# Layer 0's attention scores in the "b" banks, and a shorter given time after the delta rule's first two steps

## The chip, the cores and the metric

The kernel runs on one core of a Trainium2 chip. The metric is device time in microseconds for one execution of the whole program. The engines are TensorE (PE in the profile), VectorE (DVE), ScalarE (ACT), GpSimd (POOL) and SyncE (SP, which issues the DMAs). TensorE runs at one of two clock levels, 2.4 or 1.2 GHz; the profile gives the granted level as a share of full speed.

## What is computed

A trunk of two layers works on 256 tokens of width 2048. Each layer normalises its input, shifts and scales it by a vector computed from a condition (the "ada" product), projects it once into the inputs of three groups of heads, runs the groups, and maps their gated outputs back by one output projection.

```python
for l in range(DEPTH):
    shift, scale, gate = jnp.split(c_act @ w_ada[l] + b_ada[l], 3, axis=-1)
    h = rms_norm(x, norm_w[l]) * (1.0 + scale[:, None, :]) + shift[:, None, :]
    (gq, gk, gv, glr, gz, dq, dk, dv, da, db, dz, aq, ak, av, az) = jnp.split(h @ w_in[l], bounds, axis=-1)
    ...
    o_gla = gla_chunked(...)                  # gated linear attention, 4 heads
    ...
    o_gdn = gated_delta_chunked(...)          # gated delta rule, 4 heads, chunks of 64 tokens
    ...
    q_d = apply_rope(q_d, cos_b, sin_b)
    k_d = apply_rope(k_d, cos_b, sin_b)
    o_diff = diff_attention(q_d, k_d, v_d, lam)   # softmax(q1 k1) - lam * softmax(q2 k2), causal, 4 heads
    ...
    y = jnp.concatenate([o_gla, o_gdn, o_diff], axis=-1) @ w_out[l]
    x = x + gate[:, None, :] * y
```

Each group's output is normalised per head and multiplied by a silu gate (`z` in the kernel) ahead of the concatenation.

## The kernel before

**The main work.** Weights come from HBM in pieces of 128 x 1024 floats. ACT casts each piece to a rounded form `wh` (line 309), DVE takes the difference `wl` (line 311), and TensorE multiplies with both, three matmuls for a product: these are the matmuls into `pt`, `pf` (the input projection, `project`) and `py` (the output projection, `out_project`). DVE also makes the ada products of layer 1 during layer 0 (line 327, on pieces that a DMA brings). The output projection has three parts: the first takes the linear attention's gated output (192 matmuls), the second the delta rule's (192), the third the differential attention's (384). A part can't start until its group's gate is done (`run_until`). I call the place between two parts a barrier. Matmuls into `pt`, `pf` and `py` together are "the projection's matmuls" in what follows.

**The side work.** The three groups of heads are written as generators: `gla`, `gdn` (the delta rule), `diff_qk` (rotary step of queries and keys), `diff_attend` (scores, softmax, products), and `gate_out` (gate, transposes, split). `poll` calls them between the projection's matmuls. A generator yields either a condition or a given time `YW[i]`, in microseconds of a model clock that counts TensorE's work as it is written; it goes on when the clock is that much later. A scheduler then places each engine's instructions by a simulated timeline, with the generators' instructions at a high priority; so a given time changes the order on every engine, of instructions that lie far behind it too.

`gdn`: first, for each of the two token tiles, transposes and normalises the keys, and yields `YW[8]` behind each (line 748). Then come decays, the inverse of a triangular matrix in five levels (`Y_ps`, `Z_ps` on TensorE; DVE's lines 809 and 812; POOL's line 799), the products of queries and keys (`QK_ps`, line 795), then u and w, and the recurrence over four chunks: `wS_ps`, line 876 (`vn`), `S_ps`, line 888 (`S_gdn`). The outputs `o_gdn` of a token tile are copied by ACT (line 903), squared (line 563), and then seven POOL instructions follow one another: lines 907, 908, 909, 376 (a power), 911, 912, and 1036 of `gate_out`.

`diff_qk`: the rotary step multiplies by tables (lines 939 and 941, into the scratch `scr`), adds (line 943), and TensorE transposes the result into `ropeT_ps`. The scratch is shared with the linear attention, whose norm reads it in line 660 on POOL (after lines 657 and 376), once per token tile.

`diff_attend`: for each head and token tile a tile of scores `s_ps`, which leaves PSUM by lines 967 (DVE) and 969 (ACT), the softmax (lines 971 to 983), transposes `aT_ps` (line 989), products `o_diff`, and five small POOL instructions on `r_o` (lines 999 to 1003). Up to two tiles run at a time.

`gate_out`: line 1036 multiplies by the gate, TensorE transposes into `oT_ps`, ACT (line 1046) and DVE (line 1047) split the result for `py`.

**PSUM.** Eight banks have three tags: four of tag "p" for the projections, two of tag "a" and two of tag "b". The delta rule takes "a". The linear attention, the rotary transposes, `aT_ps` and `o_diff` take "b". `s_ps` and `oT_ps` take "a" when `free_a()` says that all of the delta rule has been written, and "b" otherwise; `free_a` speaks of what has been written, not of what has run.

Of the kernel before, what the change touches and what calls it, by code (L numbers as in the profile page):

```python
# [28 lines left out]
RAW = 1024  # L29
RAWS = 6  # L30

YW = {0: 7.0, 1: 8.0, 2: 25.0, 3: 1.25, 4: 2.0, 5: 2.0, 6: 15.0, 7: 2.5, 8: 11.25, 9: 3.25, 10: 6.0, 11: 4.0, 12: 2.94, 13: 0.75, 14: 1.5, 15: 3.0, 16: 3.0, 17: 3.5, 18: 2.0, 19: 3.75, 20: 6.25, 21: 7.5, 22: 3.75, 23: 10.0, 24: 14.0, 25: 0.75, 26: 3.75, 27: 7.0, 28: 2.25, 29: 12.0, 30: 4.2}


_SPLITS = (("gq", 256), ("gk", 256), ("gv", 512), ("glr", 16), ("gz", 512), ("dq", 512), ("dk", 512), ("dv", 512),
# [109 lines left out]
def hybrid_trunk(ctx: ExitStack, tc: tile.TileContext, x, cvec, pos, par, w_ada, w_in, w_out, w_lr, qkn, adt, cst, out):  # L145
# [23 lines left out]
    def bank(name, tag):  # L169


        return psum.tile([P, 512], F32, name=name, tag=tag, bufs=BANKS[tag])

    def tiny(name, n, bufs=2):
        return small.tile([P, n], F32, name=name, tag=name, bufs=bufs)
# [6 lines left out]
    def mm(o, lhsT, rhs, start=True, stop=True, fast=False, **kw):  # L182
        clock[0] += rhs.shape[-1] * (0.00042 if fast else 0.0017)
        return PE.matmul(o, lhsT=lhsT, rhs=rhs, start=start, stop=stop, **kw)  # L184

    def transpose(o, i):
        clock[0] += 0.11
        PE.transpose(out=o, in_=i, identity=ident)
# [82 lines left out]
    def cc(name, n=128, off=0):  # L271
        return ct[:, CST[name] + off:CST[name] + off + n]
# [102 lines left out]
    def row_power(o, v, n):  # L375
        POOL.tensor_tensor(o, v, mhalf[:, 0:n], ALU.pow)
# [170 lines left out]
    def heads(ap, n=4):  # L547
        return ap.rearrange("p (h d) -> p h d", h=n)

    def over_heads(ap, n=4, d=128):  # L550
        return ap.rearrange("p (o d) -> p o d", o=1).broadcast_to([P, n, d])
# [6 lines left out]
    def head_norm(src, n, width, r):  # L558

        for h in range(n):  # L560
            a = junk_n[0] % (256 // width) * width
            junk_n[0] += 1
            ACT.activation(junk[:, a:a + width], src[:, width * h:width * h + width], AF.Square, accum_out=r[:, h:h + 1])


    def gla(l, o, on, scr):
# [4 lines left out]
        SP.dma_start(wlr, w_lr[l])  # L571
        yield YW[0]
        pb = bank("lrT", "b")
# [3 lines left out]
        ACT.copy(lrT, pb[0:16, 0:T])  # L577
        yield YW[1]
        pz = bank("la_ps", "b")
# [21 lines left out]
        DVE.tensor_tensor(ke, gk, enb, ALU.mult)  # L601
        yield YW[2]
        pk = bank("ktT_ps", "b")
# [6 lines left out]
        for t in range(2):  # L610
            attT.append(scr[:, 4 + t])
            POOL.memset(attT[t], 0.0)
            for u in range(2):
                yield YW[3]
                pa = bank("att_ps", "b")
# [6 lines left out]
        for n in range(3):  # L622
            t, f = n // 2, 64 * (n % 2)
            yield YW[4]
            pd = bank("dS_ps", "b")
# [11 lines left out]
        for t in range(2):  # L637
            raw = scr[:, 2 * t]
            for u in range(2):
                yield YW[5]  # L640
                po = Bank(bank("o_gla", "b"))
# [311 lines left out]
    def diff_attend(l, o, g, on, scr, free_a):  # L953
        causal = cc("causal")
        qT = lambda t, i: o.aqk[:, t, 0, 128 * i:128 * i + 128]
        kT = lambda t, i: o.aqk[:, t, 1, 128 * i:128 * i + 128]
        yield YW[22]

        def one_tile(h, t, turn):
            W = 128 * (t + 1)  # L960
            pb = bank("s_ps", "a" if free_a() else "b")
            for m in range(2):
                for k in range(t + 1):
                    mm(pb[:, W * m + 128 * k:W * m + 128 * k + 128], qT(t, 2 * h + m), kT(k, 2 * h + m))
            s = scr[:, (1 + turn) % 7]
            sv, pv = heads(s[:, 0:2 * W], 2), heads(pb[:, 0:2 * W], 2)
            DVE.tensor_tensor(sv[:, :, W - 128:W], pv[:, :, W - 128:W], over_heads(causal, 2), ALU.add)
            if t == 1:
                ACT.copy(sv[:, :, 0:128], pv[:, :, 0:128])
            mxs = tiny("mx_s", 2)  # L970
            DVE.tensor_reduce(mxs, sv, AX.X, ALU.max)
            sc = g.sq[t][:, 2 * h:2 * h + 2]
            nb = tiny("nb", 2)
            DVE.scalar_tensor_tensor(nb, mxs, -1.0, sc, ALU.mult, ALU.mult)
            sm = tiny("sm", 2)
            for m in range(2):
                ACT.activation(sv[:, m, :], sv[:, m, :], AF.Exp, bias=nb[:, m:m + 1], scale=sc[:, m:m + 1],
                               accum_out=sm[:, m:m + 1])
            rsm = tiny("rsm", 2, 4)
            DVE.reciprocal(rsm, sm)  # L980
            cf = tiny("cf", 1)
            DVE.scalar_tensor_tensor(cf, sm[:, 0:1], nlam[:, l:l + 1], rsm[:, 1:2], ALU.mult, ALU.mult)
            DVE.scalar_tensor_tensor(sv[:, 0, :], sv[:, 1, :], cf, sv[:, 0, :], ALU.mult, ALU.add)
            yield YW[23]
            pa = bank("aT_ps", "b")
            for k in range(t + 1):
                transpose(pa[:, HS[k]], sv[:, 0, HS[k]])
            aT = scr[:, 7, 256 * (turn % 2):256 * (turn % 2) + 256]
            ACT.copy(aT[:, 0:W], pa[:, 0:W])
            yield YW[24]  # L990
            po = bank("o_diff", "b")[:, 0:256]
            for k in range(t + 1):
                mm(po, aT[:, HS[k]], o.av[:, k, 256 * h:256 * h + 256], k == 0, k == t)
            d = o.aqk[:, t, 0, 256 * h:256 * h + 256]
            ACT.copy(d, po)
            r = tiny("r_o", 1, 4)
            head_norm(d, 1, 256, r)
            rs = rsm[:, 0:1]
            POOL.tensor_tensor(r, r, rs, ALU.mult)
            POOL.tensor_tensor(r, r, rs, ALU.mult)  # L1000
            POOL.tensor_scalar(r, r, 1.0 / 256.0, EPS, ALU.mult, ALU.add)
            row_power(r, r, 1)
            POOL.tensor_tensor(r, r, rs, ALU.mult)
            DVE.tensor_scalar(d, d, r, None, ALU.mult)
            yield YW[25]

        running = []
        todo = [(h, t) for h in range(4) for t in range(2)]
        turn = 0
        while todo or running:  # L1010
            if todo and len(running) < 2:
                h, t = todo.pop(0)
                running.append([clock[0], one_tile(h, t, turn)])
                turn += 1
            item = min(running, key=lambda r: r[0])
            if item[0] > clock[0]:
                yield item[0] - clock[0]
                continue
            w = next(item[1], None)
            if w is None:  # L1020
                running.remove(item)
            else:
                item[0] = clock[0] + w
        for t in range(2):
            on[t] = o.aqk[:, t, 0, :]
# [64 lines left out]
    with tc.issue_after(last_fold.ins), tc.issue_after(squared.ins), tc.issue_after(spread.ins):  # L1090
# [3 lines left out]
        pb = bank("lam_ps", "a")  # L1094
# [11 lines left out]
    for l in range(L):  # L1106
# [78 lines left out]
        def free_a():  # L1185
            return run["gdn"]["done"]
# [184 lines left out]
```

## Time and profile before

| | us |
|---|---|
| three runs | 1104.52, 1107.8, 1108.89 |
| median | 1107.8 |
| the profiled execution's own time | 1106.04 |
| its span in the profile | 1103.9 |
| TensorE busy in the span | 1045.9 (95%) |
| DVE busy | 892.6 (81%) |
| ACT busy | 604.2 (55%) |
| POOL busy | 219.5 (20%) |
| mean granted clock of TensorE | 0.982 |

Times in the rows are counted from the span's start. Layer 0's projection runs up to about 434, its output projection from there to 578, and layer 1 behind it. A row of the timeline gives the start and the length of an instruction or of a run of like ones; in brackets at its end stands how long the engine was idle ahead of it, and which instruction ended that.

### The profile page before, as it was taken

The page shows a single profiled execution, that of the slowest core. Times are in us where ns is not written, and L with a number is a line of the kernel's source. Part 1 is how long each engine was busy: PE and PEld are TensorE (multiplying, and loading weights), DVE is VectorE, ACT ScalarE, POOL GpSimd, SP SyncE. Part 2 cuts the span into 40 slices and gives each one's busy share as a digit, 9 for nine tenths or more (in the row PEclk, how much of TensorE's full clock was granted, in tenths as well). Part 3 has the DMA queues.
Part 4 walks back from the last instruction along what each step waited for, and adds up shares of the span by engine and source line. Part 5 has one row for each costly group of instructions (what it writes and reads, how often), then busy time and mean ns, then how long its engine had stood idle before and what let it go on. Part 6 is the DMA issues. An engine that isn't in the chain of part 4 may idle for free.

```text
span 1103.9 us, 19674 instructions
## 1 busy us (share of the span) xinstructions
PE 1045.9 (95%) x7398; PEld 915.2 (83%) x7398; DVE 892.6 (81%) x1373; ACT 604.2 (55%) x1244; POOL 219.5 (20%) x279
## 2 busy tenths in 40 slices
PE   5989999999899989969898999999999999999998
PEld 5769888888898868959796777899899877889998
DVE  7899999989999878759768687676856878687974
ACT  4845544447655726446545555458554556557642
POOL 0000000040210941133430000014232244202400
PEclk9999999999999989969998999999999999999999
DMA  9989999988977646744578898796544656677462
GB/s 366 348 280 343 340 332 337 317 312 320 317 253 249 192 148 225 269 144 142 165 247 293 319 341 307 262 301 229 180 125 159 212 181 198 223 244 238 134 210 96
DMA packets 76799, 273.24 MB, mean 248 GB/s; under 512 B 8816, under 2 KB 9888, under 8 KB 76576
## 3 DMA queue, kind: packets, MB, share of 16 engines
q1 hardware_dynamic: 76416, 271.80, 71.8%
q8 instruction: 58, 0.95, 0.3%
q14 instruction: 37, 0.30, 0.1%
q10 hardware_dynamic: 288, 0.19, 0.1%
HBM read 267.76 MB, written 4.19 MB: 246 GB/s over the span
## 4 chain that ended last, share of the span: by engine, by line
PE 61%; DVE 16%; DMA 10%; issue 7%; ACT 3%; POOL 2%; DVEq 0%; ACTq 0%; POOLq 0%; SPq 0%
PE pt L184 30%; PE py L184 14%; PE pf L184 8%; DMA rawa<-in_w_ada 7%; DVE wl L311 5%; DVE rawa L327 4%; DMA raw<-in_w_in 2%; ACT wh L309 1%; PE Z_ps L184 1%; PE s_ps L184 1%; PE o_diff L184 1%; PE Y_ps L184 1%; PE o_gla L184 1%; DVE fr L327 1%; DVE on_gdn L673 1%
## 5 line engine op out<-in xcount | busy, mean ns | idle before, releaser
L309 ACT CAST wh<-raw 128x1024 fp32r<-128x1024 f32 (+2 forms) x310 | 318.0, 1028 | 283.4 <-PE pt L184 131.5
L311 DVE TENSOR_TENSOR wl<-raw,wh 128x1024 fp32r<-128x1024 f32 (+2 forms) x310 | 382.1, 1238 | 60.6 <-ACT wh L309 57.6
L184 PE MATMUL pt<-wl,hh 128*128 128x512 f32 (+1 forms) x768 | 293.0, 384 | 4.6 <-DVE wl L311 4.5
L327 DVE SCALAR_TENSOR_TENSOR rawa<-rawa,c_row 128x1024 f32<-128x1024 f32 x184 | 228.3, 1245 | 80.5 <-DMA rawa<-in_w_ada 79.4
L184 PE MATMUL pt<-wh,hl 128*128 128x512 f32 (+1 forms) x768 | 288.8, 380 | 1.2 <-DVE hl L403 1.2
L184 PE MATMUL pt<-wh,hh 128*128 128x512 f32 (+1 forms) x768 | 271.4, 383 | 8.4 <-ACT hh L401 4.3
L184 PEld LDWEIGHTS pt<-wh,hh 128*128 128x128 f32 x768 | 144.5, 190 | 40.8 <-ACT hh L401 5.3
L184 PEld LDWEIGHTS pt<-wl,hh 128*128 128x128 f32 x768 | 145.5, 190 | 39.2 <-DVE wl L311 10.6
L184 PEld LDWEIGHTS pt<-wh,hl 128*128 128x128 f32 x768 | 145.5, 190 | 30.1 <-DVE hl L403 2.0
L184 PE MATMUL pf<-hh,wl 128*128 128x256 f32 x512 | 143.8, 284 | 4.3 <-DVE wl L311 4.3
L184 PE MATMUL pf<-hh,wh 128*128 128x256 f32 x512 | 144.5, 283 | 1.5 <-ACT wh L309 1.5
L184 PE MATMUL pf<-hl,wh 128*128 128x256 f32 x512 | 145.4, 285 | 0.0
L184 PEld LDWEIGHTS pf<-hh,wl 128*128 128x128 f32 x512 | 96.2, 189 | 6.6 <-DVE wl L311 5.3
L184 PE MATMUL py<-ogg,wh 128*128 128x256 f32 x512 | 98.4, 288 | 0.8 <-DVE z L454 0.8
L184 PEld LDWEIGHTS pf<-hh,wh 128*128 128x128 f32 x512 | 97.1, 190 | 2.5 <-ACT wh L309 1.7
L184 PEld LDWEIGHTS pf<-hl,wh 128*128 128x128 f32 x512 | 96.9, 189 | 2.1 <-issue 1.3
L184 PE MATMUL py<-odf,wh 128*128 128x256 f32 x512 | 88.6, 278 | 2.0 <-ACT odf L1046 1.7
L184 PEld LDWEIGHTS py<-ogg,wh 128*128 128x128 f32 x512 | 80.3, 189 | 2.2 <-DVE z L454 1.2
L184 PEld LDWEIGHTS py<-odf,wh 128*128 128x128 f32 x512 | 77.3, 188 | 2.9 <-ACT odf L1046 2.1
L339 ACT ACTIVATE ada_j<-ada_p,pt 128x2 f32<-128x2 f32 x96 | 31.3, 326 | 79.2 <-DVE rawa L327 75.3
L184 PE MATMUL py<-ogg,wl 128*128 128x256 f32 x256 | 72.0, 283 | 0.0
L184 PE MATMUL py<-odf,wl 128*128 128x256 f32 x256 | 70.6, 277 | 0.0
(277 smaller groups left out, 1340.9 us busy)
## 6 DMA issues: line engine op xcount, KB each, us to landing
raw<-in_w_in SPq DMA_DIRECT2D x224, 512.0 KB, 4.9
rawa<-in_w_ada SPq DMA_DIRECT2D x184, 512.0 KB, 4.7
raw<-in_w_out SPq DMA_DIRECT2D x64, 512.0 KB, 4.4
raw<-in_w_in SPq DMA_DIRECT2D x20, 402.0 KB, 4.4
fr<-in_w_ada SPq DMA_DIRECT2D x8, 512.0 KB, 9.2
xt<-in_x SPq DMA_DIRECT2D x4, 512.0 KB, 5.8
xr<-in_x SPq DMA_DIRECT2D x4, 512.0 KB, 7.0
xs<-xr SPq DMA_DIRECT2D x1, 2048.0 KB, 7.2
```

Source lines behind the costliest of these rows:

```text
L184: return PE.matmul(o, lhsT=lhsT, rhs=rhs, start=start, stop=stop, **kw)
L309: ACT.copy(wh, raw)
L311: DVE.tensor_tensor(wl, raw, wh.bitcast(F32), ALU.subtract)
L327: DVE.scalar_tensor_tensor(raw, raw, 1.0, cb, ALU.mult, ALU.mult, accum_out=sums[:, i:i + 1])
L339: ACT.activation(tiny("ada_j", 2), sums[:, 2 * f:2 * f + 2], AF.Identity, bias=bias, scale=scale, accum_out=o)
L673: DVE.scalar_tensor_tensor(yi[:, s:T], src[:, 0:T - s], pcol("conv", w + 3 - s), yi[:, s:T], ALU.mult, ALU.add)
```

## The change

Two edits. The given time `YW[8]` goes from 11.25 to 4.0; it is yielded twice in each layer, at the end of the delta rule's two first steps. And in layer 0 a score tile takes a "b" bank always; in layer 1 it takes what it took before.

```diff
-YW = {0: 7.0, ..., 7: 2.5, 8: 11.25, 9: 3.25, ...}
+YW = {0: 7.0, ..., 7: 2.5, 8: 4.0, 9: 3.25, ...}
...
         def one_tile(h, t, turn):
             W = 128 * (t + 1)
-            pb = bank("s_ps", "a" if free_a() else "b")
+            pb = bank("s_ps", "a" if l > 0 and free_a() else "b")
             for m in range(2):
                 for k in range(t + 1):
                     mm(pb[:, W * m + 128 * k:W * m + 128 * k + 128], qT(t, 2 * h + m), kT(k, 2 * h + m))
```

No instruction is added or taken away; what changes is the order on the engines and the banks. On TensorE the two orders are the same up to the products of queries and keys of layer 0's delta rule, about 377 us in the trace. TensorE there, before (`QK_ps` and `Y_ps` of the delta rule, then the projection's matmuls into `pt`):

```order
L184 MATMUL pt<-wh,hh 128x512
L184 MATMUL pt<-wl,hh 128x512
L184 MATMUL QK_ps<-fm 64x64 x16
L184 MATMUL Y_ps<-Um,C 64x64 x16
L184 MATMUL pt<-wh,hl 128x512
L184 MATMUL pt<-wh,hh 128x512
```

and now:

```order
L184 MATMUL Y_ps<-Um,C 64x64 x12
L184 MATMUL pt<-wh,hl 128x512
L188 MATMUL ropeT_ps<-ct,scr 128x128 x8
L184 MATMUL pt<-wh,hh 128x512
L184 MATMUL pt<-wl,hh 128x512
```

The first rotary transposes stand one projection matmul behind the Y step; before, 43 of these later, between the matmuls of the next Y step. POOL at the same place, before:

```order
L657 TENSOR_SCALAR ss_gla<-ss_gla 128x4
L376 TENSOR_TENSOR ss_gla<-ss_gla,mhalf 128x4
L660 TENSOR_TENSOR mix<-scr,ss_gla 128x512
L924 TENSOR_SCALAR r_d<-r_d 128x8
L376 TENSOR_TENSOR r_d<-r_d,mhalf 128x8
L924 TENSOR_SCALAR r_d<-r_d 128x8
L376 TENSOR_TENSOR r_d<-r_d,mhalf 128x8
L831 TENSOR_TENSOR fm<-fm,ecb 128x4x128
L657 TENSOR_SCALAR ss_gla<-ss_gla 128x4
L797 MEMSET fm 128x1024
L831 TENSOR_TENSOR fm<-fm,ecb 128x4x128
L376 TENSOR_TENSOR ss_gla<-ss_gla,mhalf 128x4
```

(line 799 and the second line 660 follow) and now:

```order
L657 TENSOR_SCALAR ss_gla<-ss_gla 128x4
L376 TENSOR_TENSOR ss_gla<-ss_gla,mhalf 128x4
L657 TENSOR_SCALAR ss_gla<-ss_gla 128x4
L660 TENSOR_TENSOR mix<-scr,ss_gla 128x512
L376 TENSOR_TENSOR ss_gla<-ss_gla,mhalf 128x4
L924 TENSOR_SCALAR r_d<-r_d 128x8
L660 TENSOR_TENSOR mix<-scr,ss_gla 128x512
L376 TENSOR_TENSOR r_d<-r_d,mhalf 128x8
```

The second line 660 comes third behind the first and no longer eleventh. TensorE at the barrier between the first and the second part of layer 0's output projection, before (`S_ps`, `wS_ps`, `o_gdn` of the delta rule's last steps; `s_ps`, `aT_ps`, `o_diff` of the attention; `oT_ps` of the delta rule's gate):

```order
L184 MATMUL S_ps<-vn,kn 128x128 x4
L184 MATMUL wS_ps<-S_gdn,wT 64x128 x4
L184 MATMUL o_gdn<-vn,E 64x128 x8
L184 MATMUL o_gdn<-S_gdn,fm 64x128 x8
L184 MATMUL s_ps<-aqk 128x128 x6
L188 MATMUL oT_ps<-ct,z 128x128 x2
L188 MATMUL aT_ps<-ct,scr 128x128
L188 MATMUL oT_ps<-ct,z 128x128 x6
L188 MATMUL aT_ps<-ct,scr 128x128 x2
L184 MATMUL o_diff<-av,scr 128x256
L184 MATMUL py<-ogg,wh 128x256 x4
```

and now, from the middle of it:

```order
L184 MATMUL s_ps<-aqk 128x128 x6
L184 MATMUL o_gdn<-vn,E 64x128 x7
L184 MATMUL o_gdn<-S_gdn,fm 64x128 x8
L188 MATMUL oT_ps<-ct,z 128x128 x2
L188 MATMUL aT_ps<-ct,scr 128x128 x2
L184 MATMUL o_diff<-av,scr 128x256
L188 MATMUL aT_ps<-ct,scr 128x128
L184 MATMUL s_ps<-aqk 128x128 x2
L184 MATMUL o_diff<-av,scr 128x256 x2
L184 MATMUL s_ps<-aqk 128x128 x4
L188 MATMUL oT_ps<-ct,z 128x128 x6
L188 MATMUL aT_ps<-ct,scr 128x128
```

The attention runs ahead: the first head's scores stand inside the first part of the projection, its products here between the delta rule's steps, and further scores ahead of the gate's last transposes. On POOL seven instructions of `r_o` (lines 999 to 1001 and one line 376) stand here between line 909 and line 1036 of the delta rule's second tile, where none stood. Between this barrier and the next, the attention has 54 groups on TensorE before (18 `s_ps`, 9 `aT_ps`, 11 `o_diff`, 16 `oT_ps`) and 33 now (6, 5, 6 and 16), by the order's count of matmuls.

## Rows read from the trace of the kernel before

**Rows 1.** Busy time by stretch: start:end, length, each engine's busy us, PEclk, DMA.

```profile
396.20:406.30 10.10, 9.97 (x47) 7.19 (x47) 9.51 (x16) 2.33 (x4) 2.44 (x3) 0.50 0.55 167
471.00:494.00 23.00, 12.08 (x74) 9.61 (x74) 13.40 (x28) 8.77 (x27) 7.88 (x9) 0.65 0.48 151
578.00:592.00 14.00, 9.55 (x44) 7.42 (x44) 10.39 (x19) 7.56 (x14) 1.29 (x1) 0.76 0.76 277
800.00:1100.00 300.00, 300.00 (x2385) 268.15 (x2384) 217.07 (x331) 163.44 (x350) 72.02 (x93) 1.00 0.57 185
```

**Rows 2.** Waits of TensorE, 376 to 540: us in total, times, longest.

```profile
PE oT_ps L188 <- DVE scr L967: 4.2, 1, 4.2
...
PE py L184 <- ACT odf L1046: 1.7, 2, 1.0
...
PE oT_ps L188 <- DVE z L1036: 1.1, 1, 1.1
```

**Rows 3.** Timeline of TensorE at A: start, length, instruction, idle before and releaser.

```profile
378.94 0.51 PE L184 MATMUL pt<-wh,hl 128*128 128x512 f32 x1
...
391.29 0.39 PE L184 MATMUL pt<-wh,hh 128*128 128x512 f32 x1
395.82 0.33 PE L184 MATMUL Y_ps<-Um,C 64*64 64x64 f32 x4 [4.14 <-DVE Um L809]
```

**Rows 4.** Timeline of POOL at A.

```profile
376.71 0.20 POOL L657 TENSOR_SCALAR ss_gla<-ss_gla 128x4 f32<-128x4 f32 x1
376.99 1.04 POOL L376 TENSOR_TENSOR ss_gla<-ss_gla,mhalf 128x4 f32<-128x4 f32 x1
...
379.23 0.70 POOL L924 TENSOR_SCALAR r_d<-r_d 128x8 f32<-128x8 f32 x1
...
386.87 1.05 POOL L657 TENSOR_SCALAR ss_gla<-ss_gla 128x4 f32<-128x4 f32 x1
...
392.37 1.04 POOL L660 TENSOR_TENSOR mix<-scr,ss_gla 128x512 f32<-128x512 f32 x1
```

**Rows 5.** Timeline of DVE at A.

```profile
393.44 0.76 DVE L941 TENSOR_TENSOR scr<-aqk,rtab 128x256 f32<-128x256 f32 x2 [5.58 <-POOL mix L660]
...
395.59 0.68 DVE L943 TENSOR_TENSOR scr<-scr 128x512 f32<-128x512 f32 x1
```

**Rows 6.** Timeline of TensorE from the first barrier to the second.

```profile
470.91 1.16 PE L184 MATMUL S_ps<-vn,kn 64*128 64x128 f32 x8
...
477.19 1.96 PE L184 MATMUL o_gdn<-vn,E 64*64 64x128 f32 x14 [2.01 <-DVE vn L876]
...
487.07 0.45 PE L188 MATMUL oT_ps<-ct,z 128*128 128x128 f32 x1 [4.17 <-DVE scr L967]
...
491.65 1.49 PE L188 MATMUL oT_ps<-ct,z 128*128 128x128 f32 x6
...
493.86 0.99 PE L184 MATMUL py<-ogg,wh 128*128 128x256 f32 x2
...
537.33 0.62 PE L184 MATMUL py<-odf,wh 128*128 128x256 f32 x3 [0.67 <-ACT odf L1046]
```

**Rows 7.** Timeline of DVE at the first barrier.

```profile
485.23 1.23 DVE L327 SCALAR_TENSOR_TENSOR rawa<-rawa,c_row 128x1024 f32<-128x1024 f32 x1 [4.25 <-DMA rawa<-in_w_ada]
```

**Rows 8.** Timeline of POOL, the delta rule's last rows and the attention's.

```profile
466.00 1.24 POOL L907 TENSOR_TENSOR ss_gdn<-ss_gdn,rq 128x4 f32<-128x4 f32 x1 [33.81 <-ACT junk L563]
...
471.70 2.12 POOL L1036 TENSOR_TENSOR z<-z,on_gdn 128x512 f32<-128x512 f32 x1
483.08 0.20 POOL L907 TENSOR_TENSOR ss_gdn<-ss_gdn,rq 128x4 f32<-128x4 f32 x1 [9.25 <-ACT junk L563]
...
487.43 1.26 POOL L1036 TENSOR_TENSOR z<-z,on_gdn 128x512 f32<-128x512 f32 x1
...
515.39 2.45 POOL L1000 TENSOR_TENSOR r_o<-r_o,rsm 128x1 f32<-128x1 f32 x1
```

**Rows 9.** Busy time of the third part's projection matmuls alone, 538 to 578.

```profile
538.00:578.00 40.00, 39.72 (x345) 1.00 0.67 224
```

More of the change, by code (lines that the diff above doesn't have):

```diff
@@ L30 @@
 RAWS = 6
-YW = {0: 7.0, 1: 8.0, 2: 25.0, 3: 1.25, 4: 2.0, 5: 2.0, 6: 15.0, 7: 2.5, 8: 11.25, 9: 3.25, 10: 6.0, 11: 4.0, 12: 2.94, 13: 0.75, 14: 1.5, 15: 3.0, 16: 3.0, 17: 3.5, 18: 2.0, 19: 3.75, 20: 6.25, 21: 7.5, 22: 3.75, 23: 10.0, 24: 14.0, 25: 0.75, 26: 3.75, 27: 7.0, 28: 2.25, 29: 12.0, 30: 4.2}
+YW = {0: 7.0, 1: 8.0, 2: 25.0, 3: 1.25, 4: 2.0, 5: 2.0, 6: 15.0, 7: 2.5, 8: 4.0, 9: 3.25, 10: 6.0, 11: 4.0, 12: 2.94, 13: 0.75, 14: 1.5, 15: 3.0, 16: 3.0, 17: 3.5, 18: 2.0, 19: 3.75, 20: 6.25, 21: 7.5, 22: 3.75, 23: 10.0, 24: 14.0, 25: 0.75, 26: 3.75, 27: 7.0, 28: 2.25, 29: 12.0, 30: 4.2}
 _SPLITS = (("gq", 256), ("gk", 256), ("gv", 512), ("glr", 16), ("gz", 512), ("dq", 512), ("dk", 512), ("dv", 512),
```

## The prediction, made before the changed kernel ran

> **What bounds the kernel now.** I read the busy time by stretches first [rows 1]. From 800 us to 1100 us TensorE is busy for all of 300.00 us at full clock: the second half of layer 1 has no idle time on the engine that bounds it, so a change in what the other engines do there can only cost. Layer 0 is different: between 471 and 494 TensorE works 12.08 of 23.00 us at a mean clock of 0.65, and between 396.2 and 406.3 it is busy but at half clock (0.50, the lower of its two levels). The list of what TensorE waits for between 376 and 540 [rows 2], with the timeline [rows 3], names the places: 4.2 us for line 967 (a score tile leaving PSUM), 4.1 us for line 809 (a step of the delta rule's inverse), and 1.7 and 1.1 us for lines 1046 and 1036 (the last gate). I call them A (about 392), B (the barrier before the second part of the output projection, 471 to 494) and C (494 to 537, up to the barrier before the third part).
>
> A. TensorE ends a matmul that started at 391.29 and then waits 4.14 us [rows 3]. DVE owes it line 809, and stands itself: it waited 5.58 us for line 660 on POOL before line 941 at 393.44, which stands ahead in its order [rows 5]. On POOL the two line 660 of the two token tiles lie far apart, since other work stands between them; the second starts at 392.37 [rows 4]. The wait is followed by 10.1 us at half clock [rows 1]. Loss: 4.1 + 10.1 / 2 = 9.2 us.
>
> B. The last state update starts at 470.91 and ends about 472.06; the projection goes on at 493.86 [rows 6]: 21.8 us. In between comes the last step of the recurrence (the outputs wait 2.01 us for it at 477.19), a row of seven POOL instructions from 483.08 to 488.69 [rows 8], and the transposes of the gated output. The first of these waits 4.17 us until 487.07, for line 967: it needs a bank of the "a" pair, both hold scores, and the instruction that empties one stands on DVE behind a product that waited 4.25 us for its DMA [rows 7]. The last transposes of the gate need POOL's result of 488.69 in any case.
>
> C. From 493.86 to 537.33 [rows 6] is 43.5 us, in which 228 projection matmuls pass (the count of the order), and the rest of the attention. One such matmul costs 40.00 / 345 = 0.116 us where nothing else runs [rows 9]: 26.4 us. The waits are 1.1 for the gate and 1.7 for line 1046, in two pieces of which the last is 0.67 [rows 2, 6]: 2.8. The remaining 14.3 us are the attention's own 54 groups of scores, transposes and products.
>
> **The change part by part.** *Shorter times.* The scheduler gives the same instructions another order from the sixth step group on. The two squares of the linear attention's norm come together, so on POOL line 660 of the second tile comes six instructions after the first line 657 and not thirteen. In TensorE's order the first eight transposes of the rotary step move 43 matmuls forward, from within the Y step to right behind one matmul after it. They wait for line 943 on DVE, that one for line 941, and that one for the second line 660. POOL's first line 657 ends at 376.91. The six behind it are L376, L657, L660, L376, L924, L660: those of 1.04 us [rows 4] four times, L657 at 0.20 to 1.05 (its two rows), L924 at 0.70 or, like L657, at 0.20, and some 0.08 between each two [rows 4]: 382.0 to 383.3. On DVE come then line 941 twice (0.76), a line 327 (1.23) and line 943 (0.68) [rows 5, 7]: 384.6 to 386.0. TensorE comes to that place one matmul behind 378.94 [rows 3], at about 379.2, so it waits 5.4 to 6.8 us, longer than the 4.14 us of before, but at one place, and its wait at line 809 should be gone, since DVE is no longer held there. What the clock does then decides: the low stretches of before last 10.1 us [rows 1] and, between 578 and 592, 0.24 x 2 x 14 = 6.7 us. A part of it lies in the wait itself, where it costs nothing; the rest costs half: 0.7 to 4.1 us. Loss 6.1 to 11, I take 8.3. Gain **0.9** (between -1.8 and +3.1).
>
> *Scores in the attention's own banks.* The scores no longer hold the "a" pair, so the delta rule's steps and its gate find it free; but scores, transposed probabilities and products share the two "b" banks, so a new score tile waits for a product to leave. In the order the first head's scores now run inside the first part of the projection (+1.5 us there, with a transpose +0.2), the last state update stands six matmuls before its end (-0.7), and it ends so at about the same time as before: **0.0** with the gain of A in it.
>
> At B the transposes of the gate stand behind what POOL delivers. The chain: line 888 on DVE, and now one line 327 (1.23 [rows 7]) and one line 1262 (by the order's shape some 0.5) more before the last line 876, the outputs, ACT's copy and squares, POOL's seven, transposes, gate. Against before, the wait on line 967 is gone, but it ended 1.6 us before POOL's end and was mostly covered. Before, the transposes behind POOL's end waited for the probabilities, and the restart came 5.2 us behind POOL (488.69 to 493.86); with six transposes (1.49 at low clock [rows 6]) and one ACT and one DVE step I count 3.2: -2.0. Against it some seven of the attention's small POOL instructions that stand inside POOL's row: with 0.2 each [rows 8], one power step at half of the 1.04 that four columns take [rows 4] and 0.08 between them, +2.3. In all 21.8 - 2.0 + 2.3 and between 0 and 1.7 of DVE's two, less the 1 to 2 us that a better clock gives: **0.0** (from -1.5 to +2).
>
> At C the attention has run ahead: of its groups 33 remain of 54. By their share 14.3 x 33 / 54 = 8.7 us. The projection's matmuls stay at 26.4. The final wait doesn't go, it grows: before, 33 matmuls (3.8 us) stand in the order between the last product and the last transposes of the gate, and cover all but 1.1 of POOL's and DVE's work between them; now ten (1.2 us) stand there, so the wait may become 3.7. With the other work in between I take 2.8, and line 1046's 0.7 stays: 3.5. For small waits besides I add 1.2. 26.4 + 8.7 + 3.5 + 1.2 = 39.8, **-3.7** (from -7 to 0).
>
> *Layer 1.* The shorter times move the delta rule 25 matmuls forward there and the attention ends a little later. TensorE has no idle time to give [rows 1]: **+0.5** (0 to +2).
>
> Sum: 0.0 + 0.0 - 3.7 + 0.5 = -3.2 us. The profiled execution took 1106.0 (its span 1103.9), so it would be 1102.8; the median of the three runs, 1107.8, gives **1104.6**.
>
> **A rule against the change.** POOL's row of seven took 5.62 us at 483, where DVE waited for a DMA, and 7.82 us at 466 (to 473.82), with line 907 at 1.24 us against 0.20 [rows 8]. DVE had products and weight splits running there. The attention's line 1000 took 2.45 us in the same manner. The Trainium skill, "SBUF — State Buffer", section "Who interferes with whom", says that a DVE instruction with two inputs in SBUF contends with a GpSimd instruction that reads SBUF, and that the one that comes second blocks for the whole instruction. The trace agrees with it; by this rule the result at B would be the first rival.
>
> **The rivals.**
> 1. *Slower: POOL's row stretches.* The change puts attention work into POOL's row at B, and gives DVE work beside it. If DVE is busy there, the seven take 7.82 and not 5.62 (+2.2), and the attention's seven or eight take their long forms: two of 2.45 for 0.20 (+4.5), the rest +0.4 each (+2.4) [rows 8]. +9.1 on the sum: 1104.6 + 9.1 = 1113.7. It decides from the point where DVE works more than half of the time from POOL's first line 907 to its line 1036. For it: DVE has that work in its order. Against it: in before DVE waited for DMAs for most of that time [rows 7].
> 2. *Much faster.* The gap at B is filled by the attention, so the clock stays up and the chain itself runs faster (-2), A loses only its wait (-2.2), and the last gate is covered as in before (-2.5): 1104.6 - 6.7 = 1097.9. For it: three of the waits named go to their cause. Against it: the outputs at B still depend on one chain through four engines.
> 3. *No change.* The new wait for the first rotary transposes costs its upper end (+2.7), and the last gate's wait takes back half of C: 1104.6 + 2.7 + 1.0 = 1108.3, the time of before. For it: both waits are in the new order.
>
> **How the numbers follow.** A measurement of this kernel tells about 0.5% (5.5 us) from no change. Forecast 0.55, rival 1 0.12, rival 2 0.15, rival 3 0.18. The forecast's own bounds (-1.8 to +3.1 at A, -1.5 to +2 at B, -7 to 0 at C) give about 4 us to either side. Range **1097 to 1111**: it leaves out most of rival 1 and the far side of rival 2. Faster by over 0.5% is below 1102.3: a third of the forecast, all but a little of rival 2: 0.33. Slower by over 0.5% is above 1113.3: half of rival 1 and a tail of the third: 0.10. Within: 0.57.
>
> **What would show it.** In the changed kernel's trace: at A a wait of 5 to 7 us of the rotary transposes on line 943, at about 379 to 386, and none on line 809; a low clock for under 7 us after it. At B no wait on line 967; from the end of the last state update to the restart 20 to 24 us; POOL's row with attention in it, 8 us long. At C 40 us from restart to the third part's start, with a wait of about 3 us on line 1036. From 800 on TensorE busy throughout. Wrong would be the prediction if POOL's row took 12 us or more (rival 1), if the half clock after A stayed as long as in before with the longer wait (rival 3), or if B shrank below 19 us (rival 2).

## The result: slower by 0.6%

The changed kernel takes 1113.87 us (median of 8 runs, 1110.43 to 1116.47); the kernel before took 1107.49 in the same comparisons (8 runs). The ratio is 1.006, with a 95% interval of 1.004 to 1.008: 6.4 us slower, where I had predicted 3.2 us faster and a range that ends at 1111. The profiled execution has a span of 1111.9 us (before 1103.9) and a mean clock of 0.98.

**Where it went.** I cut both traces at the same projection matmuls of TensorE (counted from the start), so that each stretch holds the same projection work, and took the length of each:

| stretch (start in the trace of before) | before | after | difference |
|---|---|---|---|
| up to 371.9 | 371.9 | 371.9 | 0.0 |
| to the restart behind the first barrier (493.9): A and B | 121.9 | 130.9 | +8.9 |
| to the start of the third part behind the last gate (537.3): C | 43.5 | 42.7 | -0.8 |
| the third part's other 348 matmuls | 47.1 | 49.6 | +2.5 |
| layer 1 up to its third part (1056.6) | 472.2 | 467.9 | -4.3 |
| the last 384 matmuls | 43.5 | 45.2 | +1.7 |
| sum | | | +8.1 |

36 of the third part's 384 matmuls run ahead of the last gate, inside C. Two profiled executions of the same order differ by up to some 4 us (below, at e8), so the sum is 8.1 here and 6.4 in the medians.

**What TensorE waits for now**, 376 to 560 in the trace of after (total, times, longest; compare [rows 2]):

```profile
PE py L184 <- DVE z L454: 4.9, 2, 4.3
PE ropeT_ps L188 <- DVE scr L943: 4.5, 1, 4.5
PE oT_ps L188 <- DVE z L1036: 3.7, 2, 2.9
PE aT_ps L188 <- DVE scr L983: 3.3, 3, 1.6
```

Line 967, with 4.2 us the longest of [rows 2], is gone, and so is line 809's 4.14 us of [rows 3] (0.69 is left). The four longest waits are now those above; the first, third and fourth were 0.8, 1.1 and 2.7 us in before. TensorE's timeline of after shows where:

```profile
385.49 1.97 PE L188 MATMUL ropeT_ps<-ct,scr 128*128 128x128 f32 x8 [4.49 <-DVE scr L943]
...
442.57 0.58 PE L184 MATMUL py<-ogg,wh 128*128 128x256 f32 x1 [4.32 <-DVE z L454]
...
479.04 1.16 PE L184 MATMUL S_ps<-vn,kn 64*128 64x128 f32 x8
...
502.76 0.73 PE L184 MATMUL py<-ogg,wh 128*128 128x256 f32 x4
...
542.15 0.44 PE L188 MATMUL oT_ps<-ct,z 128*128 128x128 f32 x2 [2.93 <-DVE z L1036]
543.32 1.54 PE L188 MATMUL oT_ps<-ct,z 128*128 128x128 f32 x6 [0.73 <-DVE z L1036]
545.42 1.37 PE L184 MATMUL py<-odf,wh 128*128 128x256 f32 x4 [0.56 <-ACT odf L1046]
```

The first is place A, and it came much as predicted. The second stands at the end of layer 0's input projection, a place that I didn't read: line 454 is the copy of the projected gates `z` out of PSUM. The last three are C's end. What DVE did at the second place and at C's end, in its timeline of after:

```profile
437.13 0.68 DVE L454 TENSOR_TENSOR z<-pt,z 128x512 f32<-128x512 f32 x1
440.67 1.23 DVE L327 SCALAR_TENSOR_TENSOR rawa<-rawa,c_row 128x1024 f32<-128x1024 f32 x1 [2.86 <-DMA rawa<-in_w_ada]
...
441.82 0.69 DVE L454 TENSOR_TENSOR z<-pt,z 128x512 f32<-128x512 f32 x1
...
539.87 1.23 DVE L327 SCALAR_TENSOR_TENSOR rawa<-rawa,c_row 128x1024 f32<-128x1024 f32 x1 [2.50 <-DMA rawa<-in_w_ada]
...
541.02 0.35 DVE L1004 TENSOR_SCALAR aqk<-aqk,r_o 128x256 f32<-128x256 f32 x1
541.40 0.69 DVE L1036 TENSOR_TENSOR z<-z,aqk 128x512 f32<-128x512 f32 x1
```

Both times an ada product (line 327), which nothing needs before layer 1, stands in DVE's order ahead of the small step that TensorE waits for, and DVE idles 2.86 and 2.50 us for the product's DMA. The DMA is late since SP can issue it only when an earlier instruction of DVE has freed a buffer: the two issues below come right behind the end of a line 327 (436.07) and of a line 311 (535.45). SP's timeline of after:

```profile
436.10 0.33 SPq L347 DMA_DIRECT2D rawa<-in_w_ada  x1
...
535.48 0.33 SPq L347 DMA_DIRECT2D rawa<-in_w_ada  x1
```

From issue to product 4.6 us (436.10 to 440.67) and 4.4 (535.48 to 539.87) pass. In before the last two steps of line 454 ran as one pair, behind the last product that had to wait:

```profile
432.41 1.23 DVE L327 SCALAR_TENSOR_TENSOR rawa<-rawa,c_row 128x1024 f32<-128x1024 f32 x1 [2.27 <-DMA rawa<-in_w_ada]
...
434.70 1.28 DVE L454 TENSOR_TENSOR z<-pt,z 128x512 f32<-128x512 f32 x2
```

That pair was done by 436.0, in after line 454 was done by 442.5: 6.5 us later. By DVE's order 102 products stand ahead of that last step in after and 101 in before, and DVE's waits for the products' DMAs from 376 to 446 grew by about as much as the delay. In before, then in after:

```profile
DVE rawa L327 <- DMA rawa<-in_w_ada: 3.9, 4, 2.3
```

```profile
DVE rawa L327 <- DMA rawa<-in_w_ada: 10.1, 7, 2.9
```

Within or right behind each of these waits TensorE falls to its lower level. Busy time by stretch in after (the columns of [rows 1]; the clock is the sixth value behind the length):

```profile
382.70:389.50 6.80, 4.01 (x14) 3.52 (x15) 6.80 (x9) 2.75 (x6) 6.66 (x6) 0.50 0.48 153
440.70:447.50 6.80, 4.86 (x22) 4.57 (x22) 4.86 (x7) 2.83 (x5) 0.00 (x0) 0.50 0.98 378
480.20:502.80 22.60, 16.60 (x97) 12.60 (x97) 16.62 (x39) 12.01 (x44) 9.29 (x24) 0.77 0.51 163
543.10:549.90 6.80, 6.02 (x26) 5.55 (x27) 1.57 (x3) 1.27 (x2) 0.00 (x0) 0.50 0.14 58
```

The stretches at 440.7 and 543.1 are new; each is 6.8 us at 0.50. The third row is B: TensorE is busy 16.60 of 22.60 us at 0.77, where it was 12.08 of 23.00 at 0.65 [rows 1], and yet the barrier is no shorter: the additional work there is the attention's.

### The profile page after: what moved, and what is told of

Same layout as the page of the kernel before. It is cut to its first block, busy times and chain, and to the rows that moved or that the text cites. A ratio compares the mean times of both kernels' runs of the same rounds, so it can differ in the third digit from the quotient of the medians.

```text
span 1111.9 us, 19667 instructions
## 1 busy us (share of the span) xinstructions
PE 1052.0 (95%) x7398; PEld 921.5 (83%) x7398; DVE 897.7 (81%) x1373; ACT 604.9 (54%) x1244; POOL 214.7 (19%) x279
## 4 chain that ended last, share of the span: by engine, by line
PE 45%; DVE 24%; DMA 13%; issue 11%; ACT 4%; POOL 2%; DVEq 0%; ACTq 0%; POOLq 0%
PE pt L184 16%; PE py L184 13%; DMA rawa<-in_w_ada 10%; PE pf L184 8%; DVE wl L311 8%; DVE rawa L327 7%; DMA raw<-in_w_in 2%; ACT wh L309 2%; DVE aqk L454 1%; ACT junk L563 1%; PE Z_ps L184 1%; DVE z L454 1%; DVE av L454 1%; DVE hn L400 1%; PE s_ps L184 1%
## 5 line engine op out<-in xcount | busy, mean ns | idle before, releaser
L184 PE MATMUL py<-odf,wh 128*128 128x256 f32 x512 | 93.0, 284 | 0.7 <-ACT odf L1046 0.6
L184 PEld LDWEIGHTS py<-odf,wh 128*128 128x128 f32 x512 | 79.8, 192 | 1.4 <-ACT odf L1046 1.0
L1262 DVE SCALAR_TENSOR_TENSOR xr<-py,ada,xr 128x256 f32<-128x256 f32 x96 | 45.5, 479 | 35.0 <-PE py L184 34.7
```

The source lines that it names most:

```text
L1262: return DVE.scalar_tensor_tensor(xr[:, c, :], d, ada[l][:, 2, c:c + 1], xr[:, c, :], ALU.mult, ALU.add)
```

## The experiments

Theory T at the start: the given times cause the loss at the end of the projection, and the banks alone would be a gain. Later theory M: the changed order puts products that wait for a DMA ahead of the steps that TensorE needs, and the hardest of these places is the last gate. The rivals are with each run. Each run was compared with the kernel before on the same chip.

| run | median us | ratio (95%) | A and B | C | third part | layer 1 | last 384 |
|---|---|---|---|---|---|---|---|
| changed kernel | 1113.87 | 1.006 (1.004 to 1.008) | +8.9 | -0.8 | +2.5 | -4.3 | +1.7 |
| e1: times alone | 1124.56 | 1.0183 (1.0163 to 1.0203) | +3.2 | +8.5 | +2.7 | +1.1 | +1.7 |
| e2: banks alone | 1114.51 | 1.0078 (1.0061 to 1.0095) | +4.0 | -2.3 | +1.8 | +2.9 | 0.0 |
| e3: after, product behind `z` | 1112.58 | 1.0056 (1.0038 to 1.0074) | +0.4 | +5.0 | +2.9 | -5.3 | +1.7 |
| e4: before, times in layer 1 | 1105.51 | 0.9994 (0.9983 to 1.0005) | -0.3 | +0.7 | 0.0 | -1.9 | +1.7 |
| e5: after, last gate freed | 1108.74 | 1.0012 (0.9995 to 1.0029) | +8.8 | -7.2 | +2.2 | -5.0 | +1.7 |
| e6: e3 and e5 | 1111.08 | 1.0030 (1.0016 to 1.0045) | +0.9 | +2.6 | +3.6 | -2.7 | +1.7 |
| e7: before, B's gate freed | 1108.53 | 1.0002 (0.9987 to 1.0017) | -6.0 | +6.1 | +2.1 | -1.5 | 0.0 |
| e8: before, last gate freed | 1108.04 | 1.0005 (0.999 to 1.002) | +2.5 | -2.3 | +3.3 | -0.6 | 0.0 |
| e9: banks, last gate freed | 1102.35 | 0.9953 (0.9934 to 0.9971) | +4.2 | -7.9 | +0.9 | -1.3 | 0.0 |

The last five columns are stretches of the profiled executions as in the table above, against the profile of before. A difference of under some 4 us in one column isn't clear of what two executions of one order differ by. The stretch up to 371.9, where all orders are still the same, differs by -1.0 to +1.5 us, and in "A and B" 2 to 3 us of e2's, e8's and e9's difference are there by 446 us, up to where their orders are still that of before.

**e1, one edit: the given time alone.**

```diff
-            pb = bank("s_ps", "a" if l > 0 and free_a() else "b")
+            pb = bank("s_ps", "a" if free_a() else "b")
```

> The shorter times alone, with the score banks of before. Theory T (the harm is done at the end of layer 0's projection: a product of line 327 that waits for its DMA now stands between the last two of line 454 on DVE, and TensorE waits 4.3 us there and runs at half clock behind it): this kernel has the same order there as the changed one, so the wait of about 4 us on line 454 is there again; the output projection of layer 0 begins some 6 us late; layer 1 takes about 4 us less than before; in all 1108 to 1112. Rival R (the harm is done at the two barriers, by scores that share the two b banks): no harm without the banks, and layer 1's gain is left: 1102 to 1106.

1124.56 us, missed by both. The wait for `z` is the changed kernel's (4.3 us), so it comes with the given times. But the times alone cost far more: C is 8.5 us longer, with all of the attention left behind the restart (48 matmuls into `s_ps`, against 36 in before and 12 in after). At B the gate's transposes wait 6.1 us for POOL, though B as a whole is shorter than in before (18.6 us). Waits of TensorE, 425 to 560, in e1:

```profile
PE oT_ps L188 <- POOL z L1036: 6.1, 1, 6.1
PE py L184 <- DVE z L454: 4.9, 2, 4.3
```

**e2, the other edit: the banks alone.**

```diff
-YW = {..., 8: 4.0, ...}
+YW = {..., 8: 11.25, ...}
```

> The banks alone, with the given time of before. Theory T: the order up to the output projection is that of before, so the wait on line 454 stays at 0.6 us; the barriers give and take about 1 us; layer 1 is that of before: 1106 to 1110. Rival R (scores in the b banks do the harm): 1112 or more, with the first barrier or the second longer than in before by over 3 us.

1114.51 us: the time of the rival, not its mechanism, since B (22.0 us) and C (41.2) are not over 3 us longer than in before. Nor did T hold: the wait on line 454 is 2.3 us and not 0.6, as it also is in some executions of before's order (last section). So each edit alone is slower, by 1.8% and 0.8%, and both together by 0.6%: their costs don't add up, because each draws a whole order of its own. e2 ends C with two waits and a long stretch at half clock. TensorE's timeline and the busy time by stretch in e2:

```profile
535.44 0.69 PE L188 MATMUL oT_ps<-ct,z 128*128 128x128 f32 x2 [2.26 <-DVE z L1036]
...
538.49 1.54 PE L188 MATMUL oT_ps<-ct,z 128*128 128x128 f32 x6 [2.36 <-DVE z L1036]
```

```profile
535.20:545.40 10.20, 7.04 (x30) 6.17 (x31) 2.65 (x5) 1.87 (x5) 1.31 (x5) 0.50 0.18 53
```

**e3, the changed kernel with the product between the last two steps of line 454 held back.** It waits in DVE's order until line 1047 of the first gate has been issued. The scheduler then placed a second product later too: 100 stand ahead of the last step of line 454, where after has 102, and the orders part at about 430 us.

```diff
+        if late:
+            late_n[0] += 1
-        with tc.high_priority(offset=AHEAD), queued("ada"):
+        with tc.high_priority(offset=AHEAD), tc.issue_after(late[0].ins) if late_n[0] == 4 else queued("ada"):
...
+                if zoff == 0 and p == 1:
+                    late.append(e)
```

> The changed kernel with one thing moved: the one product of line 327 that stood between the last two of line 454 stands behind the gate's two of line 1047. Theory T: the wait of 4.3 us on line 454 is gone and with it most of the 6.8 us of half clock behind it: 1106 to 1108.5. Rival D (the engine is short of DMA at that place in any case, and the wait comes back at the next product): 1111 or more, with the 4 us as a wait of TensorE within 20 us of the old place.

1112.58 us, ratio 1.0056 against 1.006: next to nothing came back in the time. The time is D's, but the wait didn't come back near the old place. T's mechanism is there (the wait falls from 4.3 to 1.9 us, and the last state update starts at 470.6 and not 479.0), but what follows took most of the gain. TensorE's timeline in e3 (line numbers are 3 higher there, and in e5, e7, e8 and e9: 457 is 454, 1039 is 1036, 1050 is 1047):

```profile
438.74 0.39 PE L184 MATMUL py<-ogg,wh 128*128 128x256 f32 x1 [1.89 <-DVE z L457]
...
470.61 1.16 PE L184 MATMUL S_ps<-vn,kn 64*128 64x128 f32 x8
...
491.46 1.54 PE L188 MATMUL oT_ps<-ct,z 128*128 128x128 f32 x6 [5.37 <-POOL z L1039]
```

The restart came at 494.25, 8.5 us earlier than in after, and C, 48.4 us long against 42.7, took 5.8 of them back: 24 matmuls into `s_ps` are left behind the restart, where after has 12. So the third part starts only 2.7 us earlier (542.7 against 545.4). I read this as a start set by when the attention's last scores are through, and not by when TensorE reaches B; no run separates the two.

**e4, the kernel before with the shorter time in layer 1 alone.**

```diff
-            yield YW[8]
+            yield YW[8] if l == 0 else 4.0
```

> The kernel before with the shorter time in layer 1 only. Theory G (layer 1's 4.3 us less from its first matmul to its last barrier come from the shorter times there): 1102.5 to 1104.5. Rival H (they come from a later start of layer 1, whose weights have then run ahead): no gain, 1106.5 to 1109.

1105.51 us, no difference, between the two ranges. Layer 1 itself gains 1.9 us and loses 1.7 in its last 384 matmuls, so the times give nothing in layer 1 in all. The gain lies behind 851 us, where TensorE has no idle time: from there to the last 384, the same work takes 203.7 to 204.1 us in all six kernels with the shorter times in layer 1 and 205.8 in all five without; in e4, 32 transposes of the rotary step take 3.0 us of it, counted from start to start, and in before 4.1. So less than half of the -4.3 us of the changed kernel there is the times'. The rest lies at layer 1's start, where the waits of TensorE up to 900 us fall from 11.1 us in before to 7.7 in after; why isn't tested, and e7, with before's code in layer 1, has 8.2.

**e5, the changed kernel with the last gate freed.** The first four products behind the second barrier are held until the attention's last gate has been issued; the orders are the same up to about 514 us.

```diff
-        with tc.high_priority(offset=AHEAD), queued("ada"):
+        with tc.high_priority(offset=AHEAD), tc.issue_after(late[0].ins) if 0 < late_n[0] <= 4 else queued("ada"):
...
+                if zoff == 1024 and q == 1 and p == 1:
+                    late.append(e)
```

> The changed kernel with the first four products of line 327 behind the second barrier held back on DVE until line 1047 of the last gate is through; its order is unchanged up to about 525 us. Theory M (such products, waiting for their DMA, stand ahead of the attention's last steps on DVE, 2.5 us in the changed kernel at 539.9; the wait of TensorE of 2.9 us for the last gate's line 1036 and the 6.8 us of half clock behind it come from that): the wait falls to about 1 us, the third part starts 2 to 3 us earlier, and the low clock behind it shrinks: 1109 to 1112. Rival P (the chain through POOL and ACT from the last product of the attention to line 1036 is as long without them): the wait stays over 2 us, 1113 to 1115.

1108.74 us, a little better than M expected: its median is 1.2 us above before in its own comparison, so about 5 of the 6.4 us are gone with one cause. (Its profiled execution, 1105.64 us, is 3.1 us below its median.) The timeline of TensorE at that place in e5, and DVE's, where the product now stands behind the gate:

```profile
536.80 0.88 PE L188 MATMUL oT_ps<-ct,z 128*128 128x128 f32 x6 [0.38 <-DVE z L1039]
538.34 0.62 PE L184 MATMUL py<-odf,wh 128*128 128x256 f32 x3 [0.67 <-ACT odf L1049]
```

```profile
536.05 0.69 DVE L1039 TENSOR_TENSOR z<-z,aqk 128x512 f32<-128x512 f32 x1
...
539.65 1.21 DVE L330 SCALAR_TENSOR_TENSOR rawa<-rawa,c_row 128x1024 f32<-128x1024 f32 x1
```

2.93 and 0.73 us became 0.38, and the 6.8 us behind them run at full clock. C is 6.4 us shorter than in after; 1.5 of these lie in the first 7 us behind the restart, where the orders are still the same and after ran at half clock until 509.0. e5's busy time by stretch:

```profile
538.30:545.10 6.80, 5.90 (x42) 5.20 (x42) 6.78 (x12) 4.35 (x8) 0.00 (x0) 1.00 0.46 137
```

**e6, both holds.**

```diff
+    HOLD = (((0, 0, 1), 4, 4), ((1024, 1, 1), 1, 4))
```

> The kernel of e3_gate_first, with the same four products held back as in e5_last_gate. In e3_gate_first the output projection's first part ran level with before up to the last state update (471.8 against 472.1 us), and the second barrier then came 5.1 us later than in before, behind four waits for line 983 and the last gate; a product that waited 1.4 us for its DMA stood ahead of the attention's last scores. Theory M: these waits shrink, the third part starts 3 to 5 us earlier than in e3_gate_first: 1107 to 1109.5. Rival P (the chain itself is late, because the last scores are written late): 1111 to 1113.

1111.08 us, as P expected: worse than e5 by some 2 us. The wait for `z` is short, but the transposes at B wait 5.3 us for POOL again, the last scores are written later, and the last gate waits 2.1 and 1.9 us. Products held back also keep their buffers; that may be why a weight came 1.6 us late, which I haven't tested.

**e7, the kernel before with B's gate freed.** Three products wait behind line 1047 of the delta rule's gate.

```diff
+        with tc.high_priority(offset=AHEAD), tc.issue_after(late[0].ins) if 0 < late_n[0] <= 3 else queued("ada"):
...
+                if zoff == 512 and q == 0 and p == 1:
+                    late.append(e)
```

> The kernel before with three products of line 327 held back on DVE until line 1047 of the delta rule's gate is through, so that fewer stand between the last line 876 and line 967 at the first barrier. Theory M (the wait of 4.2 us for line 967 comes from the product that waits 4.25 us for its DMA): this wait falls under 2 us; the restart comes 1 to 3 us earlier, not more, since POOL's row ends at 488.7 in any case: 1103.5 to 1106. Rival Q (held products hold up the ring of buffers, and the weights of the second part come late): the time lost comes back as waits for line 311, 1107 to 1111.

1108.53 us, no difference: the time of Q, but not by its mechanism, since no wait of TensorE for line 311 is behind it. It asks what the wait on line 967 in [rows 6] was worth, and so also the banks' edit, which was to remove it: B shrinks from 21.8 to 17.0 us, and C grows by 6.1. Of these waits between 465 and 540 the first stands in C (3.4 us at 520.8, 1.3 at its end), the second still in B:

```profile
PE oT_ps L188 <- DVE z L1039: 4.7, 2, 3.4
PE aT_ps L188 <- DVE scr L986: 4.1, 2, 3.4
```

**e8, a control: the kernel before with e5's hold** (the same lines as e5's diff, in before).

> The kernel before, with the hold of the run with the last gate freed: the first four ada products behind the second barrier wait in DVE's order until the attention's last gate is through. Theory M (the hold helped the changed kernel because a product that waits 2.50 us for its DMA stood ahead of the last gate there): the kernel before has no such wait at that place (its product at 530.67 starts without idle time, and the gate waits for POOL), so nothing comes out of it: 1105 to 1109, ratio 0.998 to 1.002. Rival G (holding products back there is a gain in any order, by about the 5 us that it gave the changed kernel): 1101 to 1104.

1108.04 us, no difference (M). The hold is no gain in itself; it works where a waiting product stands ahead of the last gate, and in before none did. The orders in e8 are those of before up to 508 us, and yet at B's end its profile stands 3.4 us behind, and e4's, with the same order up to there, 0.8 us ahead: that much executions of one order can differ.

**e9, the banks alone with e5's hold** (e2 with the lines of e5's diff; the orders of the two are the same up to 510 us).

> The banks alone (given time 11.25 as before), with the same hold. With the banks alone the product ahead of the last gate waited 2.17 us for its DMA at 533.00, TensorE waited 2.3 and 2.4 us for line 1036, and 10.2 us at half clock followed. Theory M: the hold takes 4 to 7 us off the 1114.5 of the banks alone: 1107.5 to 1110.5. Rival L (the loss of the banks alone lies in the early part, +4.4 us up to the first barrier, and in layer 1, +2.9): 1112.5 to 1115.

1102.35 us, better than M expected, and faster than both kernels: 12.2 us below the banks alone, 4.5 below before. The stretch that was at half clock in e2 is at full clock in e9:

```profile
535.20:545.40 10.20, 9.34 (x74) 8.61 (x73) 10.20 (x15) 5.52 (x10) 2.34 (x2) 1.00 0.65 213
```

The longest wait of TensorE from 500 to 545 is 0.7 us. Against e2, C and the third part give 6.6 us in the profiles and layer 1 4.2: e2 has there a wait of 1.7 us of `QK_ps` (line 674) with 6.8 us at half clock behind it, and e9 hasn't. The code of layer 1 is the same in both, so why this wait went isn't shown.

## Why the prediction was wrong

**Place A: the mechanism right, the wait a little shorter.** Predicted were a wait of 5.4 to 6.8 us on line 943, none on line 809 and under 7 us at half clock; it was 4.49, 0.69 and 6.8. POOL's second line 660 ended at 381.84, just ahead of the 382.0 to 383.3 that I had counted. Line 943 ended at 385.44, within the range, but partly by luck: it took 1.75 us and not 0.68, beside POOL's line 831. TensorE came 1.8 us later than I had counted, since more steps stood ahead of the transposes. At 425.7 us TensorE was 2.1 us ahead of before, at the same projection matmul and with four rotary transposes fewer done (predicted 0.9, at most 3.1).

**The end of the projection: the missing term.** The step that failed is the sentence "it ends so at about the same time as before". It counted TensorE's matmuls that moved, and not DVE's order; a wait for a product's DMA ahead of line 454 is no term of the sum. DVE's timeline of before shows a wait of 2.27 us for a product shortly ahead of line 454, and 0.6 us of waiting of TensorE for it: there was no reserve. TensorE's lead of 2.1 us from A only met this earlier. The last state update started 8.1 us late (479.0 against 470.9 in [rows 6]); in e5, with the changed order up to there, it started at 478.3, in e4 and e8, with before's, at 470.8 and 474.6, and in e3, with two products fewer ahead of line 454, at 470.6. Of the 10.2 us from the lead to the lag, 3.7 are the longer wait, 2.5 the half clock from its end to 447.5, and 3.0 two waits just ahead of it (`vT_ps` on lines 816 and 837, 1.6 and 1.3; both lines stand on DVE behind a product that had waited 2.0 us for its DMA); the last 1.0 I can't place. In the time, though, this term alone is worth little: e3 removed most of it, and its median is 1.3 us below the changed kernel's. The term that e5 gave back, about 5 of the 6.4 us, is the same miss at C.

**B: the length right, the reasons half right.** 22.6 us against 21.8 (predicted 20 to 24), line 967's wait gone. Rival 1 gave 1113.7, the time that came, but its mechanism isn't what happened. POOL's row took 6.84 us with eight of the attention's instructions in it, and they kept their short forms:

```profile
493.29 0.37 POOL L907 TENSOR_TENSOR ss_gdn<-ss_gdn,rq 128x4 f32<-128x4 f32 x1 [11.89 <-ACT junk L563]
...
495.43 0.58 POOL L1000 TENSOR_TENSOR r_o<-r_o,rsm 128x1 f32<-128x1 f32 x1
...
498.71 0.19 POOL L999 TENSOR_TENSOR r_o<-r_o,rsm 128x1 f32<-128x1 f32 x1
498.86 1.27 POOL L1036 TENSOR_TENSOR z<-z,on_gdn 128x512 f32<-128x512 f32 x1
```

From the first of these to the end of the last, DVE was busy 3.64 of 6.84 us, over the half that I had named as the point of decision; and about 1.25 of these are line 974, which took 0.15 us at 491.17 and 1.26 at 498.88, beside POOL's line 1036. Only one large DVE instruction there has two inputs in SBUF, a product at 494.74 (1.23 us), and beside it line 1000 took 0.58 us instead of 0.19; the next two, line 967 (which reads PSUM) and line 971 (a reduction), left POOL alone. That is as the Trainium skill has it ("SBUF — State Buffer", "Who interferes with whom"), which speaks of two inputs in SBUF. A busy share was the wrong measure; the forms of DVE's instructions would have been the right one.

**C: the waits near the number, for another reason.** I took 39.8 us, with 3.5 for the final waits. It was 42.7, with 2.93 + 0.73 + 0.56 = 4.2 us of final waits and 1.4 for line 1047 just behind the restart. I had put the wait's cause with POOL and DVE's own work; it was a product's DMA, as e5 shows: without it the wait for the gate is 0.4 us, where I had taken 2.8, and C is 36.3 us, or 37.8 without the 1.5 us of better clock at its start, below the prediction. So that the waits came near 3.5 was luck. The half clock that follows such a wait was priced at A and not here: it costs 1.7 us of the third part, and the slower step of its matmuls (below) 1.4, of the +2.5 us.

**What DVE's product costs** was taken at A and at B as 1.23 us, its own duration; [rows 7] shows one that cost 4.25 more. This is the error behind both terms: the price of a DVE instruction that must wait for a DMA is the wait, and a moved order decides who pays it.

**Layer 1: wrong sign.** +0.5 predicted, -4.3 and +1.7 measured. "TensorE has no idle time to give" is true from 800 on; before that it has. And a change of order did more there than cost: with TensorE busy throughout, the same work from 851 us to the last part takes 1.7 us less (at e4), and the last part's step isn't a matter of idle time either.

**Two slips in the working** decide nothing: rival 3 takes 1.0 us for half of C's 3.7, and the 0.116 us a matmul of [rows 9] has a few short waits in it (the step is 0.113 or 0.118, below).

**The forecast in all.** With the last gate freed, the banks' edit gives 4.5 us (e9) where I forecast 3.2, and the shorter times on top of it cost 0.6% (e5 against e9); their profiles, which are 2.6 us apart where the medians are 6.4, have 4.6 us of cost up to the restart behind B, where the wait for `z` is, and 3.0 in the last parts of the two layers, against a gain of 3.7 in layer 1. Without the hold each edit alone is slower than before (e1, e2).

## What to carry to other kernels

When a change re-draws the order, read for each barrier what stands ahead of the awaited step on the engine that makes it, and price an instruction there that depends on a DMA with what is left of the time from the DMA's issue to its landing when the engine comes to it (here 4.4 to 4.6 us in all, of which the engine waited 2.5 to 2.9), and not at its duration alone. Hold the work that nobody needs yet behind the awaited step, at the barrier whose end isn't covered by another chain: the same hold was worth 0.5% in one order (e5), 1.2% in another (e9, a third of it in layer 1, where why isn't shown) and nothing in a third (e8). A gain at an early barrier can be lost at the next one, as in e3 and e7.

## What was not expected of the hardware

**Two steps for the same matmuls.** The output projection's matmuls of 256 columns, at full clock, without idle time, on the same tiles, follow each other every 0.113 us in some runs of them and every 0.118 us in others. Busy time by stretch of `py` alone, 1060 to 1095, in before and in after:

```profile
1060.00:1095.00 35.00, 35.00 (x311) 35.00 (x310) 5.94 (x13) 1.00 0.51 166
```

```profile
1060.00:1095.00 35.00, 34.59 (x294) 34.49 (x293) 6.55 (x14) 1.00 0.61 188
```

35.00 / 311 = 0.1125 and 34.59 / 294 = 0.1177. It is the 1.7 us of the last 384. The step changes where other matmuls or a wait interrupt the stream, and then mostly holds to its end; in e6 it goes from 0.118 to 0.113 in the middle of layer 0's third part, at 564.9 us, behind one step of 0.130. Layer 1's last part has 0.118 in all six kernels with the shorter times there and 0.113 in all five without; most of layer 0's third part has 0.113 in before, e2, e4 and e9, both in e6, and 0.118 in the others. What decides it is open; no run was made for it.

**A wait that measures the other engine's lead.** TensorE's wait for `z` at the end of layer 0's projection is 0.6 us in the profile of before and 2.6 in those of e4 and e8, whose order is the same up to there. In e4 DVE did these steps 1.3 us earlier than in before and TensorE came there earlier still (at the same projection matmul, 424.1 against 427.8 us). With the banks alone it is 2.3 and 2.4 (e2, e9), with the shorter times 4.3, 4.3 and 3.8 (after, e1, e5). So of the 3.7 us between the profiles of before and after only about 2 are the change's by these profiles, and the time at which DVE is done (434.7 to 438.1 in e4, before and e8, 442.5 in after) says more than the wait.
